# Both heads of a RWKV-7 mixer side by side on TensorE: row and column tiles grouped over two PSUM banks

## The chip, the cores and the metric

The kernel runs on one core of a Trainium2 chip. The metric is the device time of one execution in microseconds. Three executions are given as times; a further one was profiled.

In the profile, PE is TensorE (matrix products), PEld its weight loads, DVE is VectorE, ACT is ScalarE, POOL is GpSimd and SP is SyncE, which issues most transfers.

## What is computed

A two-layer encoder trunk on a sequence of 1024 frames with 1024 channels. Layer 0 has a mixer of two parallel head groups: eight RWKV-7 heads of width 64 and four gated DeltaNet heads of width 128. Layer 1 has chunked softmax attention. Each layer then has a squared-ReLU MLP and a gated embedding. The change touches the mixer of layer 0 alone, and of it the RWKV heads and the triangular inverses that both head groups use. The RWKV part of the reference:

```python
def rwkv7_group(h, dh, r, k, v, ...):
    r, k, v = [z + (token_shift(z) - z) * mu for z, mu in ...]
    w_log = -softplus(-(w0 + tanh(xw @ w1) @ w2)) - 0.5
    decay = exp(-exp(w_log))
    a = sigmoid(a0 + (xa @ a1) @ a2)
    g = sigmoid(xg @ g1) @ g2
    kk = l2norm(heads(k * k_k))
    k = k * (1.0 + (a - 1.0) * k_a)
    y = wkv7_scan(r, decay, k, v, -kk, kk * a)
    ...                                    # group norm, bonus, gate

def step(state, inp):                      # of wkv7_scan, per frame
    r_t, w_t, k_t, v_t, a_t, b_t = inp
    sa = einsum('bhij,bhj->bhi', state, a_t)
    state = state * w_t + sa b_t^T + v_t k_t^T
    return state, einsum('bhij,bhj->bhi', state, r_t)
```

## The kernel before

The scan over frames is done in chunks of 128 frames. Within a chunk everything is matrix products: a strictly lower triangular matrix N from the scaled keys, the inverse of one minus N, three masked score matrices, and a recurrence from chunk to chunk through a state of 64 by 64 for a head.

The work is cut into 16 units: 8 of RWKV and 8 of DeltaNet, in turn. A unit is one half of the sequence (512 frames, four chunks) and, for RWKV, two heads: head 0 lies on partitions 0 to 63 and head 1 on 64 to 127. Each unit goes through stages, each a Python generator: `in` (the wide input projections, out `dps`, from the activations `xg` and the split weights `whi` and `wlo`), `front`, `mid` (the inverse), `back` (scores and recurrence) and `post` (norm and gate). Six lanes run these stages for different units at the same time. `run` picks the lane whose due time is earliest, by the table `LAT` and by a clock `now` that `mm` advances for each product. The tile framework then puts the instructions of each engine in their final order and sets the waits. That order is fixed: PE works through its list strictly in turn.

Names of tiles in the rows, and what they are:

- `wa2` (in rows `wa`) and `lao`: weights and inputs of the two small LoRA products, decay on rows 0 to 63 and `a` on rows 64 to 127. The results are `psw` and `psa`, both in the bank `tp`.
- `AR`, and `Bt`, `Kt` (in rows `b`): scaled rows of both heads. `N` is made of `Bt` and `AR`, one head after the other, in bank `tp`.
- `iz`: the bank of the inverse. Its steps use tiles of 16, 32 and 64 rows: `T` and `X` for the 32-wide step, `TZ` and `F` for the 64-wide step. `N` has eight matrices (four chunks, two heads), DeltaNet's `Ng` four.
- `pm`: the bank of the scores of one head and chunk: three matrices by two products, of 128 and 256 columns. DVE masks them into `PMQ`. The `tm` tiles are transposes of `Bt` and `Kt`.
- `ch`: the bank of the recurrence. For a chunk: `W` from `PMQ` and the state `Sh`; `U` from the inverse `F` and `W`; the new state `S2` from `tm`, `Vt` (in rows `b`) and `U`. DeltaNet's recurrence uses the same bank, with the state `Sg` and the rows `KQ`.
- `py`: the output of the chunk, summed over three parts, the last two per head on 64 output columns of the array.
- `pp`: the bank of the `post` stage (`post_bank`).

Each of these banks is one buffer of 2 KB a partition. A row's `64*128` is the part of the array that a product uses: rows by columns. A product whose operands start at partition 64 uses the array's lower rows, and one whose output starts at partition 64 uses its right columns.

Of the kernel before, what the change touches and what calls it, by code (L numbers as in the profile page):

```python
# [104 lines left out]
class Trunk:  # L105
# [45 lines left out]
    def mm(self, out, lhsT, rhs, start, stop):  # L151
        n, m = 1, 1
        for c in rhs.shape[1:]:
            n *= c
        for c in lhsT.shape[1:]:
            m *= c
        if rhs.dtype == F32:
            self.now += 2 * max(n / 1200, m * 0.0007)
        else:
            self.now += max(n / 2400, m * 0.00035)  # L160
        return self.nc.tensor.matmul(out, lhsT, rhs, start=start, stop=stop)  # L161

    def tr(self, out, in_, ident):
        self.now += 0.107
# [228 lines left out]
    def inverse_end(self, Xp, B, N, F):  # L393
# [8 lines left out]
        def bank(w):  # L402
            return self.psm.tile([P, N, w], F32, tag="iz", name="iz")
# [35 lines left out]
        for i in (0, 2):  # L439
# [4 lines left out]
        yield f"inverse{N}_3"  # L444

        pt = bank(64)
        for g in range(N):
            self.tr(pt[up, g, :], F[up, g, up], self.ident[up, up])
# [2 lines left out]
        A.copy(TZ[up], pt[up])  # L451
        yield f"inverse{N}_4"
        pz = bank(64)
        for g in range(N):
# [4 lines left out]
        for g in range(N):  # L459
            self.mm(px[up, g, :], TZ[lo, g, :], F[lo, g, lo], start=True, stop=True)  # L460
        A.copy(F[up, :, lo], px[up])
        yield f"inverse{N}_6"


# [293 lines left out]
    def rwkv_front(self, p, hf, sc, raws, u):  # L758
# [12 lines left out]
        def ptile():  # L771
            return psm.tile([P, HB], F32, tag="tp", name="tp")
# [10 lines left out]
        A.activation(lw, psw, AF.Tanh, bias=self.dv["hw0"][:, p:p + 1], scale=0.5)  # L783
        V.tensor_scalar(lw, lw, -0.5 * EXPM05, -0.5 * EXPM05, op0=ALU.mult, op1=ALU.add)
# [23 lines left out]
        ta = t2()  # L808
        A.activation(ta, psa, AF.Tanh, bias=self.dv["ha0"][:, p:p + 1], scale=0.5)
        yield "rwkv_front1"  # L810
        pst = ptile()
        for c in range(4):
# [17 lines left out]
            yield ("mid", u - 2)  # L830

        N = self.mid.tile([P, 8, P], F32, tag="n8", name="N")
        for h in range(2):
            sl = slice(64 * h, 64 * h + 64)
            ps = ptile()
            for c in range(4):
                self.mm(ps[:, c * C:(c + 1) * C], Bt[sl, c * C:(c + 1) * C], AR[sl, c, 0, :], start=True, stop=True)
            for c in range(4):
                A.activation(N[:, 4 * h + c, :], ps[:, c * C:(c + 1) * C], AF.Copy, scale=cc[:, 2 * c + h:2 * c + h + 1])
            yield "rwkv_front3"  # L840
        X = self.inverse_start(N, 8)
        V.tensor_tensor(v4(Kt), v4(k2), Em, op=ALU.mult)
        r = mix(0)
# [27 lines left out]
    def rwkv_back(self, p, hf, sc, st, u):  # L871
# [5 lines left out]

        pmq = {}

        def scores(c, h):  # L880

            sl = hs[h]
            ps = psm.tile([P, 3, P], F32, tag="pm", name="pm")
            self.mm(ps[:, 0, :], Bt[sl, c * C:(c + 1) * C], AR[sl, c, 1, :], start=True, stop=True)
            self.mm(ps[:, 1:3, :], Kt[sl, c * C:(c + 1) * C], AR[sl, c].rearrange("p a t -> p (a t)"),
                    start=True, stop=True)
            d = h2.tile([P, 3, P], F32, tag="PMQ", name="PMQ", bufs=NPMQ)
            V.tensor_tensor(d, ps, self.mask3, op=ALU.mult)
            pmq[c, h] = d
# [17 lines left out]
        for c in range(4):  # L907

            Sh = h2.tile([P, 2, 64], F32, tag="Sh", name="Sh", bufs=2)
            V.scalar_tensor_tensor(Sh, S.rearrange("p (o i) -> p o i", o=1).broadcast_to((P, 2, 64)), ee[:, c:c + 1],  # L910
                                   self.blk.rearrange("p (h i) -> p h i", h=2), op0=ALU.mult, op1=ALU.mult)
            if c == 0:
                yield "rwkv_back3"
            Sf = Sh.rearrange("p h i -> p (h i)")
            pw = psm.tile([P, HB], F32, tag="ch", name="ch")
            for h in range(2):
                self.mm(pw[:, hs[h]], pmq[c, h][:, 1, :], Vt[:, c, hs[h]], start=h == 0, stop=False)
            self.mm(pw[:, 0:P], AR[:, c, 0, :], Sf, start=False, stop=True)
# [9 lines left out]
            V.tensor_tensor(U.rearrange("p (h i) -> p h i", h=2), pu[:, 0:P].rearrange("p (h i) -> p h i", h=2),  # L928
                            cc[:, 2 * c:2 * c + 2].rearrange("p (h o) -> p h o", o=1).broadcast_to((P, 2, 64)),
                            op=ALU.mult)  # L930
            yield "rwkv_back5"
# [10 lines left out]
            py_c = py[:, c * C:(c + 1) * C]  # L942
            self.mm(py_c, Sf, AR[:, c, 1, :], start=True, stop=False)
            for h in range(2):
                self.mm(py_c[hs[h]], Vt[:, c, hs[h]], pmq[c, h][:, 2, :], start=False, stop=False)
                self.mm(py_c[hs[h]], U[:, hs[h]], pmq[c, h][:, 0, :], start=False, stop=True)
            yield "rwkv_back6"
        G.tensor_scalar(self.S[f"r{p}"], S, ee[:, 4:5], None, op0=ALU.mult)

# [1004 lines left out]
```

## Time and profile before

| what | value |
|---|---|
| three runs | 3192.11, 3194.34, 3196.0 us (median 3194.34) |
| the profiled execution | 3200.01 us, span 3198.3 us |
| PE busy over the span | 3102.1 us (97%), 17576 records |
| DVE, ACT, POOL busy | 2013.2, 1384.2, 531.5 us |
| the mixer of layer 0 | from the start to about 970 us |
| granted TensorE clock, mean | 0.974 |

The layer 0 mixer takes about 30% of the span; the rest is the output projection, the MLP, the embedding gate and layer 1, which the change leaves alone. Busy time is the time that at least one instruction of the engine is under way. Records of PE overlap their neighbours (a record lasts longer than the distance to the next), so what a product costs is read from the starts.

### The profile page before, as it was taken

Reading aid. Unit: us, or ns where it says so; the run is one execution under the profiler, and the core shown is the slowest. Engines: PE = TensorE matmul, PEld = TensorE weight load, DVE = VectorE, ACT = ScalarE, POOL = GpSimd, SP = SyncE. Lnnn points to the kernel's source line nnn. Section 1 sums busy time; section 2 is a strip of 40 time slices with the busy share of each in tenths; the row PEclk is TensorE's granted clock in tenths of the full one; section 3 lists DMA queues with packets and bytes.
Section 4 is the critical chain, followed back from the end, with each engine's and each line's share of the span. In section 5 each row is a group of like instructions: output and inputs, shape, how many; then the busy total and the mean of one; then the engine's idle time right before and its main releaser. Section 6 shows DMA issues by size and latency. Waiting matters only on the chain.

```text
span 3198.3 us, 46044 instructions
## 1 busy us (share of the span) xinstructions
PE 3102.1 (97%) x17576; PEld 2565.6 (80%) x17576; DVE 2013.2 (63%) x4020; ACT 1384.2 (43%) x2608; POOL 531.5 (17%) x978
## 2 busy tenths in 40 slices
PE   7999999999999999999999898999899999999999
PEld 5777777777777888888888888988778888888887
DVE  6566675556748666655546576776768666655552
ACT  4333333334326555322123477777756555312121
POOL 6334442433410000000004211010110000000002
PEclk8999899999899999999999999999999999999999
DMA  3322112212325433523213210110156433522213
GB/s 120 94 63 60 47 46 67 70 61 70 129 95 194 155 119 108 192 93 106 92 51 128 70 36 32 45 41 16 69 177 209 150 121 109 185 105 92 106 47 105
DMA packets 144716, 309.60 MB, mean 97 GB/s; under 512 B 40944, under 2 KB 43120, under 8 KB 144496
## 3 DMA queue, kind: packets, MB, share of 16 engines
q1 hardware_dynamic: 126064, 273.10, 25.6%
q10 hardware_dynamic: 18432, 33.56, 2.7%
q8 instruction: 138, 2.26, 0.3%
q14 instruction: 82, 0.67, 0.1%
HBM read 232.16 MB, written 74.45 MB: 96 GB/s over the span
## 4 chain that ended last, share of the span: by engine, by line
PE 85%; DVE 7%; ACT 3%; DMA 2%; issue 1%; POOL 0%; SPq 0%; ACTq 0%; DVEq 0%; POOLq 0%
PE dps L161 70%; PE ch L161 3%; PE iz L161 2%; PE pm L161 2%; PE tp L161 1%; PE po L161 1%; PE py L161 1%; DVE ptile L318 1%; PE pt L165 1%; DMA wraw<-in_w_qkv 1%; PE sn L161 1%; PE pp L161 1%; DVE pb L1795 1%; PE sc L161 1%; ACT pb L1808 1%
## 5 line engine op out<-in xcount | busy, mean ns | idle before, releaser
L161 PE MATMUL dps<-r,act 128*128 128x512 f32 x3528 | 824.4, 392 | 0.0
L161 PEld LDWEIGHTS dps<-r,act 128*128 128x128 f32 x3528 | 662.1, 188 | 145.7
L161 PE MATMUL dps<-xg,whi 128*128 128x512 f32 x1280 | 438.2, 418 | 11.7 <-ACT xg L320 7.3
L161 PE MATMUL dps<-late,act 128*128 128x512 f32 x1536 | 352.9, 391 | 0.0
L161 PEld LDWEIGHTS dps<-late,act 128*128 128x128 f32 x1536 | 288.4, 188 | 63.1
L161 PE MATMUL dps<-wq,act 128*128 128x384 f32 x1536 | 304.8, 344 | 5.8 <-DVE vs L1704 3.1
L1452 POOL TENSOR_TENSOR pn<-pn,prs 128x512 f32<-128x512 f32 x32 | 45.5, 1426 | 1590.7 <-ACT prs L354 1496.3
L161 PEld LDWEIGHTS dps<-xg,whi 128*128 128x128 f32 x1280 | 248.4, 199 | 75.2 <-issue 10.7
L161 PEld LDWEIGHTS dps<-wq,act 128*128 128x128 f32 x1536 | 265.6, 191 | 10.4 <-DVE vs L1704 5.1
L161 PE MATMUL dps<-xg,wlo 128*128 128x512 f32 x640 | 266.4, 416 | 3.1 <-DVE wlo L277 3.1
L1328 DVE TENSOR_TENSOR late<-late,dps 128x512 f32<-128x512 f32 x224 | 152.9, 685 | 150.1 <-PE dps L161 119.2
L1427 DVE TENSOR_TENSOR xw<-xw,dps 128x512 f32<-128x512 f32 x192 | 131.5, 685 | 148.4 <-PE dps L161 145.5
L1226 ACT CAST act<-act 128x1024 fp32r<-128x1024 f32 (+1 forms) x99 | 94.8, 964 | 285.2 <-DMA act<-in_w 124.2
L1226 ACT CAST act<-late 128x512 fp32r<-128x512 f32 x210 | 124.5, 618 | 135.9 <-PE dps L161 117.0
L1227 DVE TENSOR_TENSOR act<-late,act 128x512 fp32r<-128x512 f32 x210 | 139.9, 687 | 26.1 <-ACT act L1226 25.9
L161 PEld LDWEIGHTS dps<-xg,wlo 128*128 128x128 f32 x640 | 126.9, 198 | 34.1 <-issue 4.8
L161 PE MATMUL dps<-xw,act 128*128 128x512 f32 x576 | 138.9, 392 | 0.0
L276 ACT CAST whi<-wraw 128x1024 fp32r<-128x1024 f32 x78 | 81.7, 1047 | 124.2 <-PE dps L161 74.4
L161 PEld LDWEIGHTS dps<-xw,act 128*128 128x128 f32 x576 | 108.1, 188 | 24.1
L1227 DVE TENSOR_TENSOR act<-act 128x1024 fp32r<-128x1024 f32 (+1 forms) x99 | 109.9, 1115 | 21.0 <-ACT act L1226 19.8
L161 PE MATMUL po<-ptile,vs 128*128 128x256 f32 (+1 forms) x576 | 104.9, 297 | 17.1 <-DVE ptile L318 7.7
L277 DVE TENSOR_TENSOR wlo<-wraw,whi 128x1024 fp32r<-128x1024 f32 x78 | 101.4, 1301 | 25.6 <-ACT whi L276 25.6
(472 smaller groups left out, 5369.4 us busy)
## 6 DMA issues: line engine op xcount, KB each, us to landing
act<-in_w SPq DMA_DIRECT2D x68, 512.0 KB
hd<-late ACTq DMA_DIRECT2D x128, 256.0 KB
late<-in_w SPq DMA_DIRECT2D x60, 512.0 KB
wraw<-in_w_in SPq DMA_DIRECT2D x56, 512.0 KB
act<-hd SPq DMA_DIRECT2D x56, 512.0 KB
wraw<-in_w_out SPq DMA_DIRECT2D x21, 512.0 KB
wraw<-in_w_qkv SPq DMA_DIRECT2D x21, 512.0 KB
pn<-pnd SPq DMA_DIRECT2D x32, 256.0 KB
```

What stands on the lines that cost most here:

```text
L161: return self.nc.tensor.matmul(out, lhsT, rhs, start=start, stop=stop)
L165: return self.nc.tensor.transpose(out, in_, ident)
L276: nc.scalar.copy(hi, raw)
L277: nc.vector.tensor_tensor(lo, raw, hi.bitcast(F32), op=ALU.subtract)
L318: nc.vector.tensor_tensor(dst[:, 1, sl], src, dst[:, 0, sl].bitcast(F32), op=ALU.subtract)
L1226: A.copy(hi, s)
L1227: V.tensor_tensor(lo, s, hi.bitcast(F32), op=ALU.subtract)
L1328: V.tensor_tensor(r, t, u, op=ALU.add)
L1427: V.tensor_tensor(x[n][:, sl], x[n][:, sl], ps, op=ALU.add)
L1452: G.tensor_tensor(pn, pn, prs[:, sl], op=ALU.mult)
L1795: V.tensor_tensor_reduce(S, pn[:, 0:nn * P], toep[:, (3 - nn) * P:], op0=ALU.add, op1=ALU.max, scale=1.0, scalar=NEG, accum_out=mx[:, 0:1])
L1808: A.activation(S, S, AF.Exp, bias=mx[:, 2:3], accum_out=l[:, 0:1])
```

## The change

Products that use different parts of the array are issued in turn, so that they can be under way together.

- `together` ties a list of products in order (an ordering edge without a semaphore).
- The two LoRA products become one pair: `psa` (rows 64 to 127) goes to the bank `pp` and `psw` to `tp`. The stop `rwkv_front0` goes.
- N of both heads becomes one tied group of eight products, head 1 in `pp` and head 0 in `tp`, alternating by chunk. One stop `rwkv_front3` instead of two.
- The scores of a chunk become one tied group for both heads: head 1 in `pp`, head 0 in `pm`. They are all issued at the chunk before, after its state; before, head 0's came after `W` and head 1's after the state. The stop `rwkv_back0` goes.
- The state and the output products of a chunk are written head by head within each step, and the output's first part comes before the stop `rwkv_back5`.
- In the inverse, the 32-wide step alternates its two tiles, and the 64-wide step puts every other matrix in the upper half of the bank. Its result is then copied by two ACT instructions (even and odd matrices) instead of one.

The number of products, their shapes and their precision stay as they were.

```diff
+    def together(self, products):
+        edge = mybir.DependencyInfo(mybir.DependencyClass.NoSync, mybir.DependencyReason.DATA)
+        for u, v in zip(products, products[1:]):
+            self.tc.add_manual_dep(v.ins, u.ins.name, edge, reason="together")
...
-        for i in (0, 2):
-            for g in range(N):
+        for g in range(N):
+            for i in (0, 2):
                 self.mm(pz[quad[i + 1], g, :], B[quad[i], g, quad[i + 1]], T2[quad[i], g, :], start=True, stop=True)
...
+        def both(ps, f):
+            for g in range(N):
+                f(ps[up if g % 2 == 0 else lo, g, :], g)
+        def out(dst, ps):
+            for e, r in ((0, up), (1, lo)):
+                A.copy(part(dst, e), part(ps[r], e))
...
         pz = bank(64)
-        for g in range(N):
-            self.mm(pz[lo, g, :], B[up, g, lo], TZ[up, g, :], start=True, stop=True)
-        A.copy(TZ[lo], pz[lo])
+        both(pz, lambda o, g: self.mm(o, B[up, g, lo], TZ[up, g, :], start=True, stop=True))
+        out(TZ[lo], pz)
...
-        psw = ptile()
-        self.mm(psw, self.wa2[0:64, p * P:(p + 1) * P], sc["lwa"][0:64], start=True, stop=True)
+        psw, psa = ptile(), self.post_bank()
+        self.together([self.mm(ps, self.wa2[r, p * P:(p + 1) * P], sc["lwa"][r], start=True, stop=True)
+                       for ps, r in ((psa, slice(64, 128)), (psw, slice(0, 64)))])
...
-        yield "rwkv_front0"
-        psa = ptile()
-        self.mm(psa, self.wa2[64:128, p * P:(p + 1) * P], sc["lwa"][64:128], start=True, stop=True)
...
-        for h in range(2):
-            sl = slice(64 * h, 64 * h + 64)
-            ps = ptile()
+        pn = [ptile(), self.post_bank()]
+        ms = []
+        for c in range(4):
+            for h in (1, 0):
+                sl = slice(64 * h, 64 * h + 64)
+                ms.append(self.mm(pn[h][:, c * C:(c + 1) * C], Bt[sl, c * C:(c + 1) * C], AR[sl, c, 0, :],
+                                  start=True, stop=True))
+        self.together(ms)
...
-        def scores(c, h):
...
+        def scores(c):
+            cs = slice(c * C, (c + 1) * C)
+            ps = [psm.tile([P, 3, P], F32, tag="pm", name="pm"), self.post_bank()[:, 0:3 * C].rearrange("p (a t) -> p a t", a=3)]
+            ms = [self.mm(ps[h][:, 0, :], Bt[hs[h], cs], AR[hs[h], c, 1, :], start=True, stop=True) for h in (1, 0)]
+            ms += [self.mm(ps[h][:, 1:3, :], Kt[hs[h], cs], AR[hs[h], c].rearrange("p a t -> p (a t)"),
+                           start=True, stop=True) for h in (1, 0)]
+            self.together(ms)
+            for h in (1, 0):
+                d = pmq[c, h] = h2.tile([P, 3, P], F32, tag="PMQ", name="PMQ", bufs=NPMQ)
+                V.tensor_tensor(d, ps[h], self.mask3, op=ALU.mult)
-        scores(0, 0)
-        yield "rwkv_back0"
-        scores(0, 1)
+        scores(0)
...
-            if c < 3:
-                scores(c + 1, 0)
...
-            for h in range(2):
-                self.mm(pu2[hs[h], 0:64], Ktm[:, c, hs[h]], Vt[:, c, hs[h]], start=True, stop=False)
-                self.mm(pu2[hs[h], 0:64], Btm[:, c, hs[h]], U[:, hs[h]], start=False, stop=True)
+            for t, v in ((Ktm, Vt[:, c]), (Btm, U)):
+                for h in range(2):
+                    self.mm(pu2[hs[h], 0:64], t[:, c, hs[h]], v[:, hs[h]], start=t is Ktm, stop=t is Btm)
+            for v, j in ((Vt[:, c], 2), (U, 0)):
+                for h in range(2):
+                    self.mm(py_c[hs[h]], v[:, hs[h]], pmq[c, h][:, j, :], start=False, stop=j == 0)
...
             if c < 3:
-                scores(c + 1, 1)
+                scores(c + 1)
```

More of the change, by code (lines that the diff above doesn't have):

```diff
@@ L438, in inverse_end @@
         px = bank(32)
-        for i in (0, 2):
-            for g in range(N):
+        for g in range(N):
+            for i in (0, 2):
                 self.mm(px[quad[i], g, :], Z[quad[i + 1], g, :], X2[quad[i + 1], g, :], start=True, stop=True)
@@ L444, in inverse_end @@
         yield f"inverse{N}_3"
+        part = lambda t, e: t[:, e::2, :]
+        def both(ps, f):
+            for g in range(N):
+                f(ps[up if g % 2 == 0 else lo, g, :], g)
+        def out(dst, ps):
+            for e, r in ((0, up), (1, lo)):
+                A.copy(part(dst, e), part(ps[r], e))
         pt = bank(64)
@@ L453, in inverse_end @@
         pz = bank(64)
-        for g in range(N):
-            self.mm(pz[lo, g, :], B[up, g, lo], TZ[up, g, :], start=True, stop=True)
-        A.copy(TZ[lo], pz[lo])
+        both(pz, lambda o, g: self.mm(o, B[up, g, lo], TZ[up, g, :], start=True, stop=True))
+        out(TZ[lo], pz)
         yield f"inverse{N}_5"
         px = bank(64)
-        for g in range(N):
-            self.mm(px[up, g, :], TZ[lo, g, :], F[lo, g, lo], start=True, stop=True)
-        A.copy(F[up, :, lo], px[up])
+        both(px, lambda o, g: self.mm(o, TZ[lo, g, :], F[lo, g, lo], start=True, stop=True))
+        out(F[up, :, lo], px)
         yield f"inverse{N}_6"
@@ L832, in rwkv_front @@
         N = self.mid.tile([P, 8, P], F32, tag="n8", name="N")
-        for h in range(2):
-            sl = slice(64 * h, 64 * h + 64)
-            ps = ptile()
+        pn = [ptile(), self.post_bank()]
[7 more added lines that the diff above has]
+        for h in (1, 0):
             for c in range(4):
[L837 to L840, printed above, removed]
+                A.activation(N[:, 4 * h + c, :], pn[h][:, c * C:(c + 1) * C], AF.Copy, scale=cc[:, 2 * c + h:2 * c + h + 1])
+        yield "rwkv_front3"
         X = self.inverse_start(N, 8)
@@ L878, in rwkv_back @@
         pmq = {}
-        def scores(c, h):
[L882 to L889, printed above, removed]
-        scores(0, 0)
-        yield "rwkv_back0"
-        scores(0, 1)
+        def scores(c):
[5 more added lines that the diff above has]
+            self.together(ms)
+            for h in (1, 0):
+                d = pmq[c, h] = h2.tile([P, 3, P], F32, tag="PMQ", name="PMQ", bufs=NPMQ)
+                V.tensor_tensor(d, ps[h], self.mask3, op=ALU.mult)
+        scores(0)
         yield "rwkv_back1"
@@ L930, in rwkv_back @@
                             op=ALU.mult)
+            py_c = py[:, c * C:(c + 1) * C]
+            self.mm(py_c, Sf, AR[:, c, 1, :], start=True, stop=False)
             yield "rwkv_back5"
             pu2 = psm.tile([P, HB], F32, tag="ch", name="ch")
-            for h in range(2):
-                self.mm(pu2[hs[h], 0:64], Ktm[:, c, hs[h]], Vt[:, c, hs[h]], start=True, stop=False)
-                self.mm(pu2[hs[h], 0:64], Btm[:, c, hs[h]], U[:, hs[h]], start=False, stop=True)
+            for t, v in ((Ktm, Vt[:, c]), (Btm, U)):
[4 more added lines that the diff above has]
+                    self.mm(py_c[hs[h]], v[:, hs[h]], pmq[c, h][:, j, :], start=False, stop=j == 0)
             S2 = h2.tile([P, 64], F32, tag="S2", name="S2", bufs=2)
@@ L940, in rwkv_back @@
             if c < 3:
-                scores(c + 1, 1)
[L942 to L946, printed above, removed]
+                scores(c + 1)
             yield "rwkv_back6"
```

4 lines of the change are left out of this document (2 added, 2 removed).

## The prediction

> **What bounds the kernel now.** I read the page first. TensorE (PE) is busy for 97% of the span, so the page alone says only that the matrix engine's list sets the end.
>
> ```profile
> span 3198.3 us, 46044 instructions
> PE 3102.1 (97%) x17576; PEld 2565.6 (80%) x17576; DVE 2013.2 (63%) x4020; ACT 1384.2 (43%) x2608; POOL 531.5 (17%) x978
> ```
>
> The change touches only the mixer of layer 0, which ends near 970 us. So the second view is the busy time by stretch: length, then PE, PE's weight loads, VectorE (DVE), ScalarE (ACT), GpSimd (POOL), and then the granted clock.
>
> ```profile
> 120.00:970.00 850.00, 831.76 (x6666) 649.86 (x6665) 525.76 (x1220) 309.76 (x626) 316.12 (x700) 0.94 0.23 72
> 970.00:3198.00 2228.00, 2168.98 (x10486) 1837.29 (x10484) 1418.86 (x2686) 1028.64 (x1907) 149.07 (x128) 0.99 0.30 105
> ```
>
> In the mixer's 850 us PE idles 850 - 832 = 18 us, while the other engines have much room. PE's list is the bound: a microsecond off it is a microsecond off the end, as long as no wait takes its place. The granted clock is 0.94 here against 0.99 later.
>
> The third view is the groups of PE instructions by form (count, busy us, mean ns of one). A float32 product is two records.
>
> ```profile
> L161 PE MATMUL pm<-AR,b 64*128 64x256 f32 x128 | 40.3, 395 | 0.0
> L161 PE MATMUL pm<-AR,b 64*128 64x128 f32 x128 | 31.3, 325 | 0.5 <-DVE PMQ L888 0.5
> L161 PE MATMUL tp<-AR,b 64*128 64x128 f32 x128 | 19.8, 295 | 1.5 <-DVE cc L815 1.5
> L161 PE MATMUL tp<-lao,wa 64*128 64x512 f32 x32 | 18.0, 641 | 0.5 <-ACT f L783 0.4
> L161 PE MATMUL iz<-X,T 32*32 32x32 f32 x384 | 17.4, 199 | 0.0
> L161 PE MATMUL iz<-T,N 32*32 32x32 f32 x256 | 9.8, 193 | 0.0
> L161 PE MATMUL iz<-T,Ng 32*32 32x32 f32 x128 | 4.9, 194 | 0.0
> L161 PE MATMUL iz<-F,TZ 64*64 64x64 f32 x192 | 14.7, 222 | 0.0
> L161 PE MATMUL iz<-TZ,N 64*64 64x64 f32 x128 | 9.3, 221 | 0.0
> L161 PE MATMUL iz<-TZ,Ng 64*64 64x64 f32 x64 | 6.0, 237 | 0.0
> ```
>
> These are what the change regroups: the scores (pm, 64 head groups of four records), the matrix N (tp from AR), the two small LoRA products (tp from lao) and the inverses' last steps (iz). Each uses a part of the array.
>
> What two parts do side by side, PE's timeline shows at 577 us (start, time from first start to last end, count). There a LoRA product on rows 64 to 127 of the array happens to stand beside a score group on rows 0 to 63, in another bank.
>
> ```profile
> 576.69 0.51 PE L161 MATMUL iz<-F,TZ 64*64 64x64 f32 x6
> 577.13 0.69 PE L161 MATMUL tp<-lao,wa 64*128 64x512 f32 x1
> 577.13 0.70 PE L161 MATMUL pm<-AR,b 64*128 64x128 f32 x3
> ...
> 578.18 0.50 PE L161 MATMUL dps<-xg,whi 128*128 128x512 f32 x1
> ```
>
> Both start at 577.13, and the next wide product starts 1.05 us later. That is what the two LoRA records need alone (18.0 us for 32, so 1.1 for two). The score group cost nothing: the change's mechanism, in the kernel before.
>
> **What it takes off PE's list.** The prices are read from PE's timeline at 922 and at 904 us.
>
> ```profile
> 922.26 0.40 PE L161 MATMUL dps<-xg,wlo 128*128 128x512 f32 x1
> 922.49 0.62 PE L161 MATMUL dps<-xg,whi 128*128 128x512 f32 x2
> 923.05 0.92 PE L161 MATMUL pm<-AR,b 64*128 64x128 f32 x4
> 923.90 0.59 PE L161 MATMUL iz<-T,Ng 32*32 32x32 f32 x16
> 924.41 0.50 PE L161 MATMUL dps<-xg,wlo 128*128 128x512 f32 x1
> 924.75 0.40 PE L161 MATMUL dps<-xg,whi 128*128 128x512 f32 x1
> 925.08 0.34 PE L161 MATMUL ch<-b,tm 128*64 128x64 f32 x4
> 925.24 0.29 PE L161 MATMUL ch<-U,tm 128*64 128x64 f32 x4
> 925.36 0.28 PE L161 MATMUL py<-PMQ,U 128*64 128x128 f32 x1
> ...
> 925.59 0.38 PE L161 MATMUL py<-PMQ,U 128*64 128x128 f32 x2
> 925.90 0.50 PE L161 MATMUL dps<-xg,whi 128*128 128x512 f32 x1
> ```
>
> ```profile
> 904.03 1.14 PE L161 MATMUL iz<-F,TZ 64*64 64x64 f32 x16
> 905.10 0.49 PE L161 MATMUL py<-AR,Sh 128*128 128x128 f32 x2
> ```
>
> Wide records follow each other at 0.23 us (922.26 to 922.49). The group at 923.05 starts 0.10 late after the second one of 922.49, lasts 0.85 to the next start, and the first wide product after a change of tile size takes 0.34 (924.41 to 924.75), 0.11 too long. So a head's scores cost 0.10 + 0.85 + 0.11 = 1.06 us.
>
> 1. Scores: 64 x 1.06 = 68 us now, 32 pairs x 1.06 = 34 then. In the order, 18 of the 32 pairs stand whole. The other 14 have something else inside, mostly behind head 1's first product, which then pays its own entry, exit and two records, some 0.4 us each, 6 in all. It saves 28.
> 2. N: 19.8 us in 16 head groups, half of it goes: 10.
> 3. LoRA: 1.1 us each, seven of eight pairs adjacent: 8, less 2 for places like 577 us: 6.
> 4. The output py: after the pairing, head 1's last two records no longer run alone. They start at 925.59, and the 0.31 to 925.90 less 0.09 of a change is 0.22, times 32 chunks: 7.
> 5. The inverses' 64-wide steps: 16 records take 1.07 us (904.03 to 905.10), so about 0.058 each without the change. 384 records are 22 us; run on two column halves, 11 go.
> 6. The 32-wide steps: 16 records take 0.51 (923.90 to 924.41), 0.024 each without the change. Alternating tiles I take at two thirds, 0.016; 768 records: 6.
>
> Sum 68 us. With tails and shared changes counted otherwise I get 58 to 78. The count of tile-size changes in PE's order agrees in direction: 632 before, 515 after, up to the mixer's end.
>
> First place of the order: N of the second RWKV unit on PE, before (head 0's four products with one bank; head 1's stand 16 rows on).
>
> ```order
> L161 MATMUL dps<-xg,wlo 128x512
> L161 MATMUL tp<-AR,b 128x128 x4
> L161 MATMUL ch<-W,F_224 128x64 x2
> L161 MATMUL iz<-T_1742,Ng 32x16 x16
> L161 MATMUL dps<-xg,whi 128x512 x2
> ```
>
> The same unit on PE after, head 1 in the bank pp and head 0 in tp.
>
> ```order
> L161 MATMUL iz<-TZ,N 64x64 x8
> L161 MATMUL pp<-AR,b 128x128
> L161 MATMUL tp<-AR,b 128x128
> L161 MATMUL pp<-AR,b 128x128
> L161 MATMUL tp<-AR,b 128x128
> L161 MATMUL pp<-AR,b 128x128
> L161 MATMUL tp<-AR,b 128x128
> L161 MATMUL pp<-AR,b 128x128
> L161 MATMUL tp<-AR,b 128x128
> L161 MATMUL dps<-xg,whi 128x512 x2
> ```
>
> The heads now alternate, so each product has its partner beside it.
>
> **What it gives back: waits.** The answers of DVE, ACT and POOL stay as long as they were. Where PE's own work between a product and the reader of its result was a score group, that cover shrinks. Second place: PE in the recurrence of the third chunk of the second RWKV unit, before.
>
> ```order
> L161 MATMUL pm<-AR,b 128x128
> L161 MATMUL pm<-AR,b 128x256
> L161 MATMUL ch<-Sh,AR 128x128
> L161 MATMUL py<-AR,Sh 128x128
> L161 MATMUL py<-PMQ,b 64x128
> L161 MATMUL ch<-W,F_224 128x64 x2
> L161 MATMUL pm<-AR,b 128x128
> L161 MATMUL pm<-AR,b 128x256
> L161 MATMUL ch<-b,tm 64x64
> L161 MATMUL ch<-U,tm 64x64
> ```
>
> The same chunk on PE after.
>
> ```order
> L161 MATMUL pp<-AR,b 128x256
> L161 MATMUL pm<-AR,b 128x256
> L161 MATMUL ch<-b,tm 64x64 x2
> L161 MATMUL ch<-U,tm 64x64 x2
> L161 MATMUL py<-PMQ,U 64x128 x2
> L161 MATMUL ch<-b,PMQ 128x64 x2
> L161 MATMUL ch<-Sh,AR 128x128
> L161 MATMUL py<-AR,Sh 128x128
> L161 MATMUL py<-PMQ,b 64x128 x2
> L161 MATMUL ch<-W,F_224 128x64 x2
> L161 MATMUL ch<-b,tm 64x64 x2
> L161 MATMUL ch<-U,tm 64x64 x2
> ```
>
> Before, a score group stands between the product that makes U (ch from W and F) and the rows that need U (ch from b and tm, ch from U and tm). After, nothing does. What that costs, the trace shows at 943 us, where it happens once already.
>
> ```profile
> 943.40 0.66 PE L161 MATMUL ch<-W,F 128*128 128x64 f32 x4
> 944.44 0.34 PE L161 MATMUL ch<-b,tm 128*64 128x64 f32 x4 [0.38 <-DVE U L928]
> ```
>
> The four records take 0.11 each, so of the 1.04 us some 0.55 is lost. I went through the five kinds of recurrence step of both head groups in both orders and priced PE's work between maker and reader with the rows above. Steps with under 0.8 us of cover: 12 before, 42 after. So 30 x 0.55 = 16 us come back for certain. The recurrences are about 210 of PE's 656 rows that wait for another engine. If the others lose cover alike, it is 16 x 656 / 210 = 51. I take 40, nearer to the upper end, because the others include two new kinds of wait: the one bank pp now serves the post stage, the second LoRA product, N and the scores, and PE, strictly in order, holds all wide products behind a row that waits for pp's last reader (VectorE's masks and the post stage's products); and the inverse's copies are split in two.
>
> **The clock.** In the mixer the clock is at half for a part of the time, as the busy time by stretch shows.
>
> ```profile
> 538.00:541.40 3.40, 3.40 (x71) 2.94 (x74) 2.44 (x17) 1.75 (x3) 0.45 (x2) 1.00 0.49 154
> 541.40:544.80 3.40, 3.40 (x25) 2.35 (x24) 3.12 (x20) 0.37 (x1) 2.18 (x5) 0.50 0.02 5
> 544.80:548.20 3.40, 3.40 (x9) 2.35 (x8) 1.45 (x3) 0.00 (x0) 0.70 (x1) 0.50 0.00 0
> ```
>
> ```profile
> 546.72 0.63 PE L161 MATMUL dps<-xg,wlo 128*128 128x512 f32 x1
> 547.15 1.05 PE L161 MATMUL dps<-xg,whi 128*128 128x512 f32 x2
> ```
>
> Wide records then follow at 0.43 instead of 0.23, so one such stretch of 3.4 us costs 1.7. The stretch before the drop (538.00) has PE busy for all 3.40 us, but with small tiles. More waits make more lean stretches, shorter small-tile runs make fewer. I take 5 more, 8 us, between 0 and 10 more (17 us). [...]
>
> Costed at nothing: the tie itself (no instruction), the split copies (ACT works 310 of 850 us; uncovered, 32 x 0.15 would be 5 us, which the 51 holds), and the front's removed stops. N's transfer on SP's queue waits for the same eight ACT copies as before.
>
> **The sum.** -68 + 40 + 8 = -20 us. The profiled execution took 3200.0 us, its span 3198.3. It lies 0.2% over the median of the runs, 3194.3, so I take the difference from that median: 3174.
>
> **The rivals.**
> A, the waits eat it. Place: PE rows that wait for the bank pp and the recurrences. Price 0.55 us each; beyond 110 new waits, 60 us, the gain is gone. With 75 us it ends at 3194 - 68 + 75 + 8 = 3209. For it: 658 of PE's rows wait for another engine after the change, and no wide product can pass one of them. Against: PE idles only 18 us now. Chance 0.13.
> B, the waits stop at the counted 16 and the clock stays: -52, 3142. For it: most steps in the order still have over 2 us of cover. Chance 0.15.
> C, column halves of one row range don't overlap, so terms 4 and 5 fail: -68 + 18 + 40 + 8 = -2, 3192. Against: at 925.08 eight column-half records take 0.28 us to 925.36, half of eight times 0.058. [...] Chance 0.05.
> D, row halves pair at 577 us but not when both load 128 columns at each step: terms 1 to 3 shrink to the saved tile-size changes, about 20, with 24 from the rest; then the new order's waits (40) and the clock (17) win: +13, 3207. For it: no row shows two such streams in step. Chance 0.04.
>
> **How the numbers follow.** The forecast, 3174, has 0.63, with a range of its own of 3158 to 3190. A measurement of this kernel can tell about 0.2%, 6 us, from no change. Faster: 0.60 of the forecast's 0.63 and B's 0.15, with a bit of C: 0.76. Same: C and the forecast's edge, 0.09. Slower: A and D, less their near edges: 0.15. The range reaches to near B's 3142, at 3145, and on the other side to 3200, short of A and D.
>
> **What would show it.** Right: score, N and LoRA groups of both heads within one run of about 1.06, 1.2 and 1.1 us, two records starting together; PE's busy time in the mixer down by 30 us or more while its idle time rises from 18 to 30 or more; waits of half a microsecond for U, W, S2 and pp. Wrong: pairs that last twice as long (D), 64-wide steps still at 0.058 a record (C), idle time under 25 us (B) or over 70 (A).

## The result: slower by 0.9%, and the profile after

The changed kernel takes 3224.8 us (median of six executions, 3215.1 to 3233.2) against 3193.6 us for the kernel before (six executions, 3192.1 to 3196.1). The ratio is 1.0089, with a 95% interval of 1.0073 to 1.0105. The forecast was 3174, in a range of 3145 to 3200: wrong, and wrong in sign. The profiled execution took 3223.7 us, its span is 3222.0 us.

The head of the page after, span and engines, answers the first fence of the prediction. PE is still busy nearly throughout, but by 43 us less.

```profile
span 3222.0 us, 46099 instructions
PE 3059.5 (95%) x17576; PEld 2537.6 (79%) x17576; DVE 2011.8 (62%) x4020; ACT 1389.1 (43%) x2640; POOL 528.5 (16%) x978
```

The busy time by stretch, the mixer after 120 us and the rest of the span: first the kernel before.

```profile
120.00:967.00 847.00, 830.98 (x6664) 649.36 (x6663) 523.67 (x1217) 309.14 (x625) 316.12 (x700) 0.94 0.23 72
967.00:3198.00 2231.00, 2169.76 (x10487) 1837.80 (x10486) 1420.95 (x2688) 1029.26 (x1908) 149.07 (x128) 0.99 0.30 105
```

The same two stretches after; the mixer now ends at 992 us.

```profile
120.00:992.00 872.00, 793.98 (x6679) 621.78 (x6677) 522.61 (x1217) 314.66 (x657) 313.41 (x700) 0.90 0.23 70
992.00:3222.00 2230.00, 2168.15 (x10487) 1840.51 (x10486) 1419.62 (x2688) 1028.89 (x1908) 147.03 (x128) 0.99 0.31 105
```

The rest of the span is as long as it was (2231 and 2230 us). All the loss is in the mixer, 25 us longer, and it can be split in three. PE's idle time rises from 847 - 831 = 16 us to 872 - 794 = 78 us, by 62. The granted clock falls from 0.94 to 0.90: by the clock records of the two traces it is at half for 101 us before and 172 after. Of these, PE is idle for 7 and 26 us, which stand in the idle time already. In the other 95 and 147 us it works at half clock and loses half of them, 47 and 73 us, so 26 more. What is left, PE's own work at full clock, falls from 784 to 721 us. So 25 = -63 + 62 + 26, where the prediction had -68 + 40 + 8. The change took off nearly what it was to take off, and the two terms that give back were both too small.

The -63 is seen in PE's timeline after (start, time to the last end). First a LoRA pair, then the scores of both heads.

```profile
271.99 0.69 PE L161 MATMUL pp<-lao,wa 64*128 64x512 f32 x1
271.99 0.69 PE L161 MATMUL tp<-lao,wa 64*128 64x512 f32 x1
...
273.05 0.44 PE L161 MATMUL iz<-T,Ng 32*32 32x32 f32 x16
273.89 0.37 PE L161 MATMUL pp<-AR,b 64*128 64x128 f32 x1 [0.40 <-ACT f L798]
273.89 0.37 PE L161 MATMUL pm<-AR,b 64*128 64x128 f32 x1
...
274.74 1.05 PE L161 MATMUL tp<-hsel,f 128*128 128x2 f32 x8
```

Both LoRA products take 273.05 - 271.99 = 1.06 us, as one did before, and both heads' scores 274.74 - 273.89 = 0.85, the time of one head. The partners start together to 0.01 us. Column halves run side by side too, in the inverse's 64-wide step:

```profile
358.68 0.68 PE L161 MATMUL iz<-TZ,N 64*64 64x64 f32 x16
359.29 0.51 PE L161 MATMUL dps<-xg,whi 128*128 128x512 f32 x1
```

Sixteen records take 0.61 us, where 1.07 stood before. Rivals C and D are out.

The 62 us of idle time, in the view of PE's waits after (from 120 us to the mixer's end: total, times, longest):

```profile
PE iz L161 <- ACT T L416: 11.4, 7, 3.3
PE ch L161 <- DVE U L941: 10.1, 10, 2.3
PE ch L161 <- DVE S L957: 5.0, 12, 1.4
PE ch L161 <- DVE Sg L1128: 4.6, 5, 2.4
PE ch L161 <- DVE Sh L925: 4.5, 5, 1.3
```

U, the states S, Sg and Sh are the recurrence, as foreseen, but a wait for U is 1.0 us long (10.1 / 10); at the place that the prediction took its price of 0.55 from, the row shows 0.38. The longest was not foreseen: the first step of an inverse, which waits for `T`. The timeline of all engines shows such a place.

```profile
257.06 0.60 POOL L392 COPY sub<-sub 32x256 f32<-32x256 f32 x1
...
257.69 0.33 SPq L394 DMA_DIRECT2D z<-sub  x1
...
258.44 1.05 PE L161 MATMUL pp<-ones,o 128*128 128x1 f32 x8 [1.17 <-ACT o L1135]
...
259.36 0.47 PE L161 MATMUL py<-AR,Sh 128*128 128x128 f32 x2
259.37 0.37 SPq L396 DMA_DIRECT2D Xp<-z  x1
...
262.43 0.35 ACT L416 ACTIVATE T<-Xp,half 128x64 f32<-128x64 f32 x1 [3.52 <-DMA Xp<-z]
262.83 0.63 PE L161 MATMUL iz<-T,Ng 32*32 32x16 f32 x32 [3.01 <-ACT T L416]
263.39 1.22 PE L161 MATMUL dps<-xg,whi 128*128 128x512 f32 x2
264.41 0.63 PE L161 MATMUL dps<-xg,wlo 128*128 128x512 f32 x1
264.84 1.05 PE L161 MATMUL dps<-xg,whi 128*128 128x512 f32 x2
```

POOL ends the small 16-wide inverses at 257.66, two transfers carry them through memory to 262.4, and PE, which got there early, stands for 3.0 us with wide products next in its list. Then the wide products run at 0.43 us each (264.41 to 264.84). The busy time of these stretches shows why:

```profile
256.50:259.90 3.40, 2.10 (x14) 1.71 (x14) 1.38 (x4) 1.61 (x4) 1.02 (x3) 1.00 0.29 70
259.90:263.30 3.40, 0.47 (x32) 0.47 (x32) 2.49 (x14) 0.35 (x1) 0.46 (x1) 0.52 0.40 123
263.30:266.70 3.40, 3.40 (x21) 2.69 (x13) 0.00 (x0) 0.31 (x1) 0.00 (x0) 0.50 0.00 0
```

In the first, PE works 2.1 of 3.4 us, 0.9 us of it on the one-column products of 258.44; the clock falls in the second and still holds PE back in the third, which is full. So this wait is paid twice, once as 3.0 us of idle time and once in the clock behind it (0.43 us a wide product instead of 0.23). Counted from the clock records after 100 us, the mixer falls to half clock 14 times before and 22 times after.

### The profile page after: what moved, and what is told of

Same layout as the page of the kernel before. It is cut to its first block, busy times and chain, and to the rows that moved or that the text cites. A ratio compares the mean times of both kernels' runs of the same rounds, so it can differ in the third digit from the quotient of the medians.

```text
span 3222.0 us, 46099 instructions
## 1 busy us (share of the span) xinstructions
PE 3059.5 (95%) x17576; PEld 2537.6 (79%) x17576; DVE 2011.8 (62%) x4020; ACT 1389.1 (43%) x2640; POOL 528.5 (16%) x978
## 4 chain that ended last, share of the span: by engine, by line
PE 73%; DVE 9%; ACT 4%; DMA 4%; POOL 2%; issue 2%; SPq 0%; DVEq 0%; POOLq 0%; ACTq 0%
PE dps L161 63%; PE ch L161 2%; PE po L161 1%; PE pp L161 1%; PE iz L161 1%; POOL subt L389 1%; PE pt L171 1%; DVE ptile L324 1%; PE sn L161 1%; DMA wraw<-in_w_qkv 1%; POOL sub L391 1%; DMA Xp<-z 1%; DVE pb L1809 1%; ACT pb L1822 1%; DMA yr<-yd 1%
## 5 line engine op out<-in xcount | busy, mean ns | idle before, releaser
L161 PE MATMUL dps<-xg,whi 128*128 128x512 f32 x1280 | 445.4, 425 | 23.7 <-ACT xg L326 7.5
```

## Experiments

For every execution there is a time, a span and a mean granted clock. So a time can be split without a trace: span x (1 - clock) is what the half clock costs at most (idle time at half clock counts in it), and the remainder of the median time is called rest. The columns are medians of each version. The ratio is to executions of the kernel before that ran beside that version; the row before has the 31 that ran beside e1 to e4. PE's idle time is that of the mixer in the profiled execution, good to some 3 us by where its end is set, and the profiled execution is not always a typical one (3185 us for e1, 3221 for e3).

| version | us | ratio to before, 95% | clock | half clock costs | rest | idle |
|---|---|---|---|---|---|---|
| before | 3197.0 | 1 | 0.973 | 86 | 3111 | 16 |
| the change | 3224.8 | 1.0089 (1.0073 to 1.0105) | 0.9575 | 137 | 3088 | 78 |
| e1 inverses alone | 3196.7 | 1.0000 (0.9987 to 1.0014) | 0.972 | 89 | 3107 | 21 |
| e2 LoRA and N alone | 3200.5 | 1.0011 (0.9995 to 1.0027) | 0.9695 | 98 | 3103 | 19 |
| e3 scores alone | 3212.5 | 1.0044 (1.0029 to 1.0060) | 0.9675 | 104 | 3108 | 38 |
| e4 state and output alone | 3204.9 | 1.0023 (1.0010 to 1.0036) | 0.971 | 93 | 3112 | 24 |
| e5 head after head | 3226.4 | 1.0097 (1.0077 to 1.0116) | 0.9605 | 127 | 3099 | 60 |
| e6 filler | 3209.0 | 1.0047 (1.0029 to 1.0065) | 0.970 | 96 | 3113 | 57 |
| e7 N, inverses, state | 3166.2 | 0.9910 (0.9893 to 0.9928) | 0.9745 | 81 | 3085 | 27 |
| e8 scores in tp | 3191.9 | 0.9976 (0.9959 to 0.9993) | 0.965 | 112 | 3080 | 54 |
| e9 old scores | 3203.3 | 1.0017 (1.0006 to 1.0029) | 0.9625 | 120 | 3083 | 30 |
| e10 pairs behind W, in tp | 3163.5 | 0.9900 (0.9885 to 0.9915) | 0.9715 | 90 | 3073 | 39 |
| n1 before, other order | 3196.5 | 1.0000 (0.9990 to 1.0009) | 0.975 | 80 | 3117 | 19 |
| e11 e9 with the stop | 3176.1 | 0.9936 (0.9917 to 0.9955) | 0.9685 | 100 | 3076 | 24 |
| e12 e7 without the stop | 3178.1 | 0.9942 (0.9923 to 0.9960) | 0.970 | 95 | 3083 | 21 |
| e13 before with filler | 3213.4 | 1.0056 (1.0031 to 1.0080) | 0.975 | 80 | 3133 | 23 |
| e14 e10, other order | 3162.0 | 0.9893 (0.9872 to 0.9914) | 0.971 | 92 | 3070 | 34 |
| e15 change with the stop | 3228.9 | 1.0104 (1.0074 to 1.0134) | 0.958 | 136 | 3093 | 68 |
| e16 e10 in pp | 3197.8 | 1.0007 (0.9984 to 1.0029) | 0.966 | 109 | 3089 | 61 |

**The parts by themselves (e1 to e4).** Each puts one part of the diff into the kernel before: e1 the hunks of `inverse_end`, e2 those of LoRA and N, e3 `scores` and its calls, e4 the lines from `py_c` to `S2`.

> The kernel before with the change to the inverses alone (32-wide steps alternate, 64-wide steps on two column halves, split copies). Two theories for the 30 us by which the whole change is slower. Cover theory: the groups save what the prediction took, and the loss comes from the recurrence steps that lost their cover and from the shared bank pp, so not from here: 3194 - 17 = 3177, at most 5 more for the split copies. Order theory: any edit that puts PE's list in a new order costs some 25 us of waits and half clock, wherever the edit is: 3194 - 17 + 25 = 3202.

> The kernel before with the LoRA pair and the group of N alone (both in banks tp and pp, two stops gone). Cover theory: -16 and some waits for pp, 3180 to 3188. Order theory: -16 + 25, 3203.

> The kernel before with the paired scores alone (both heads after the chunk's state, banks pm and pp). Cover theory: nearly all the loss is here, -28 + 55 = +27, 3221. Order theory: -28 + 25, 3191.

> The kernel before with the new order of the state's and the output's products alone (scores stay head by head at their old places). Cover theory: -7 and a little given back, 3187 to 3191. Order theory: -7 + 25, 3212.

Both theories fell. Cover fits e3 roughly (3212) but not e1 (3197), order fits e2 (3200) and not e3, and neither fits e4 (3205). No part gains. They add 0, 3, 16 and 8 us, 27 together, about what the whole loses. The split shows what they share: the half clock costs more in each (3, 12, 18, 7 us) while the rest hardly falls. Yet each part does take off what it should. Split like the mixer above, by the clock records of the profiled executions, PE's work at full clock falls by 13, 15, 25 and 11 us in e1 to e4, where the prediction had 17, 16, 28 and 7. These add up to 64, and the whole change takes off 63. So the savings add, and in each part waits and clock took them back. From here on the clock was the first theory.

**Unpairing in place (e5).** The scores, and N in the same way:

```diff
-            ms = [self.mm(ps[h][:, 0, :], Bt[hs[h], cs], ...) for h in (1, 0)]
-            ms += [self.mm(ps[h][:, 1:3, :], Kt[hs[h], cs], ...) for h in (1, 0)]
+            ms = []
+            for h in (1, 0):
+                ms += [self.mm(ps[h][:, 0, :], ...), self.mm(ps[h][:, 1:3, :], ...)]
```

> The changed kernel with the products of the scores and of N tied head after head instead of in turn (all of head 1, then all of head 0); banks, places and everything else as in the change. Time is split here into a part at full clock (time less span times one minus the mean granted clock) and the rest, which the half clock costs. Changed kernel: 3225, of it 3089 and 136. Pairs save: the full-clock part rises by the 28 + 10 us that the prediction gave to scores and N, to 3127, and the total to 3255 to 3270. Pairs save nothing: no change, 3225.

It gave 3226, the rest 11 us more. That is no answer to whether pairs save, because the edit did not unpair. PE's timeline of e5 for N, where all four products of head 1 (pp) are listed ahead of head 0's (tp):

```profile
292.90 0.82 PE L161 MATMUL pp<-AR,b 64*128 64x128 f32 x5
293.45 0.37 PE L161 MATMUL tp<-AR,b 64*128 64x128 f32 x1
293.56 0.27 PE L161 MATMUL pp<-AR,b 64*128 64x128 f32 x1
...
293.89 0.72 PE L161 MATMUL tp<-AR,b 64*128 64x128 f32 x5
294.54 0.49 PE L161 MATMUL py<-AR,Sh 128*128 128x128 f32 x2
```

Head 0's first record starts at 293.45, ahead of head 1's sixth at 293.56: here PE starts a product ahead of three records that stand before it in the list and use the other rows. The group takes 1.64 us. In the change it takes 1.09, as its timeline shows.

```profile
292.86 0.37 PE L161 MATMUL pp<-AR,b 64*128 64x128 f32 x1
292.87 0.37 PE L161 MATMUL tp<-AR,b 64*128 64x128 f32 x1
...
293.95 0.34 PE L161 MATMUL ch<-U,tm 128*64 128x64 f32 x4
```

The scores, four records a head, ran as pairs as before.

**The clock: filler (e6, e13).** Added work that nobody reads, behind U's product:

```diff
             for h in range(2):
                 self.mm(pu[:, hs[h]], X[:, 4 * h + c, :], W[:, hs[h]], start=True, stop=True)
+            nc.tensor.matmul(pu[:, P:3*P], self.ident, self.mask3[:, 0:2, :], start=True, stop=True)
```

> The changed kernel with added work: behind each RWKV product that makes U, one float32 product of the full array, 128 by 256, into unused columns of the bank ch, read by no one: 32 x 0.44 = 14 us more for PE. Clock theory (half clock follows stretches in which the array does little, and is the main loss): granted clock up from 0.958 by 0.003 or more, and the time no longer than 3225 in spite of the work. Waits theory (the loss is idle time): the filler stands in the waits for U, 10 us, the rest is added: 3229 with the clock as it was.

> The kernel before with the same filler as in the changed kernel (32 float32 products of the full array behind U's products, 14 us of work that nobody reads). Clock theory: where scores stand behind U already, the clock has less to gain: full-clock part up by 14 to 20, half-clock share down by 5 to 15, so 3197 to 3211, no gain as in the changed kernel (-16). If the filler helps for another reason: 3180 or less.

With 14 us more to do, the changed kernel is 16 us faster (3209; the two ratios' intervals do not touch): the half clock costs 96 us instead of 137, the rest is 25 longer. Idle time at half clock is in the 41 us between them. Split by the clock records of the two profiled executions, PE's work rises by 23 us, its idle time falls by 21 (the waits for U from 10.1 to 4.6, those for `T` from 11.4 to 3.0), and the half clock while PE works costs 17 less. So work can buy back both losses here, and the clock is not the whole gain. In the kernel before, the same filler costs 16 us, a little more than expected, and the clock has only 6 to give. The filler can move the order too, so the gain need not come from the filled waits alone.

**The clock by itself (c_clock).** Ahead of the kernel before, stretches of float32 products of the full array: 128-column ones ("wide") mixed evenly with one-column ones, then chains of wide products that wait for ScalarE. `product` issues one of them and ties it to the one before.

```diff
+for share in (12, 9, 7, 5):
+    for i in range(110):
+        if (i + 1) * share // 20 > i * share // 20:
+            product(d[:, 0:P], self.ones)
+        else:
+            product(t[:, 0:1], self.ones[:, 0:1])
+    dense(50)
+for k in (4, 2, 1):
+    x = self.ones
+    for _ in range(96 // (k + 2)):
...
+        for _ in range(k):
+            product(d[:, 0:P], x)
...
+        nc.scalar.copy(x, d[:, 0:P])
+    dense(50)
```

> The kernel before with a row of test stretches on PE ahead of everything, some 250 us: products of the full array, 128 by 128 columns, mixed evenly with products of one column, PE busy throughout, with shares of 60, 45, 35 and 25% of the wide ones; then chains of 4, 2 and 1 wide products, each chain waiting for ScalarE's copy of its result, so with gaps well under 1 us and PE in use for about two thirds, a half and a third; 50 wide products between stretches. Activity theory: the clock is granted in full at 60% and two thirds, and falls to half at 25% and at a third; the border shows where. [...]

One execution took 3520 us. The busy time by stretch; the clock is the number behind POOL's.

```profile
18.00:42.00 24.00, 24.00 (x216) 24.00 (x216) 0.00 (x0) 1.56 (x3) 0.00 (x0) 1.00 0.07 23
54.00:77.00 23.00, 23.00 (x208) 23.00 (x208) 0.00 (x0) 0.00 (x0) 0.00 (x0) 1.00 0.01 1
...
93.60:137.70 44.10, 44.10 (x208) 44.10 (x209) 0.00 (x0) 0.00 (x0) 0.00 (x0) 0.50 0.00 1
148.00:187.00 39.00, 39.00 (x200) 39.00 (x199) 0.00 (x0) 0.00 (x0) 0.00 (x0) 0.54 0.00 0
202.00:225.00 23.00, 16.95 (x118) 14.10 (x118) 0.00 (x0) 3.98 (x15) 0.00 (x0) 1.00 0.00 1
238.00:250.00 12.00, 7.70 (x44) 5.61 (x44) 0.00 (x0) 2.65 (x10) 0.00 (x0) 1.00 0.00 0
251.00:270.00 19.00, 14.48 (x51) 11.24 (x51) 0.00 (x0) 3.12 (x12) 0.00 (x0) 0.50 0.00 0
286.00:315.00 29.00, 20.13 (x52) 12.76 (x52) 0.00 (x0) 6.62 (x25) 0.00 (x0) 0.50 0.00 1
```

In the first four rows PE is busy throughout. With 60 and 45% of wide products the clock is granted in full. With 35% it is at half from 93.6 us on (the stretch began at 89.2), and with 25% soon too. A record takes 24.0 / 216 = 0.111 us. So the chains of four wide products use the array for 118 x 0.111 / 23 = 57% and keep the clock. Those of two use it for 44 x 0.111 / 12 = 41%, with gaps of only (12 - 7.7) / 11 = 0.4 us; they keep it for 12 us and lose it between 250 and 251 us. Those of one run at half clock. So in this run the border lies between 35 and 45% where the rest is thin work, and below 57% where it is idle time. The clock records place it more closely. In them the clock changes only at steps of 3.41 us (so too in the traces before and after), and in such steps the chains of two start 13, 12, 12 and 11 records: it falls after the one with 11 (11 x 0.111 / 3.41 = 36%), not after 12 (39%). The stretch of 35% has 11 wide records in the step before its fall. In these falls PE has no gap, or gaps of 0.4 us.

Much the same border is found in the mixer. For each step of 3.41 us at full clock, PE's records were added up, each at the time measured for its columns (0.111 us for 128, or 0.23 us for 512 in the wide projections) times the share of the array's rows and columns that it uses. This was done in the traces of both kernels and of all other versions, from 100 us to near the mixer's end. Of the 311 steps after which the clock fell, 298 use under 37% of the array; of the 3684 after which it stayed, 32 do. Without the share of rows and columns the two kinds mix: the best border then has 141 steps on the wrong side, and 41 with it. The traces of before and after alone have 36 such falls, 34 of them under 37%, and 398 steps after which the clock stayed, 4 of them; the best border there has 15 steps on the wrong side without the share, and 3 with it.

**Which part brings it: scores (e7 to e10, e16).** e7 has N, the inverses and state and output changed, scores and LoRA as before; e9 adds the LoRA pair, with the stop `rwkv_front0` gone as in the change; e8 is the change with the LoRA products as before and

```diff
-            ps = [psm.tile([P, 3, P], F32, tag="pm", name="pm"), self.post_bank()[...]...]
+            ps = [psm.tile([P, 3, P], F32, tag="pm", name="pm"), psm.tile([P, HB], F32, tag="tp", name="tp")[...]...]
```

e10 is e8 with the call moved, and e16 is e10 with `post_bank()` again.

```diff
             A.copy(W, pw[:, 0:P])
+            if c < 3:
+                scores(c + 1)
...
             S = S2
-            if c < 3:
-                scores(c + 1)
```

> The change without its scores part and without the LoRA pair (both as before): paired N, the inverses and the new order of state and output. If the parts simply add up as measured one by one (inverses -1, N and LoRA +3, state and output +8): 3204 to 3208. If the loss sits in the paired scores' place and bank and in the LoRA pair's earlier start: -10 -17 -7 on PE's list with some 12 us of waits: 3175.

> The change with head 1's scores in the bank tp instead of pp, and the LoRA products apart as before. Shared-bank theory (pp, which the post stage, N and the scores share, makes the waits that bring the half clock): the waits shrink by 15 to 20 us and the clock recovers to 0.967 or more, 3185 to 3200. If the place of the scores behind the state is what matters, not the bank: 3215 to 3225.

> The changed kernel with its scores part undone (head by head, head 0's after W, head 1's after the state, bank pm); N, LoRA, inverses, state and output stay changed. If the scores' new place and bank make the loss: near the version without the LoRA pair, 3166 to 3178, granted clock 0.972 or more. If the LoRA pair and its earlier start hold a part of it: 3185 to 3200.

> The change with the paired scores of the next chunk issued right after W's product (where head 0's were before), head 1's in the bank tp, and the LoRA products apart as before. Cover theory: the pair hides W's copy again and the waits fall below the 54 us of the version with the pair behind the state (3192): clock 0.970 or more, 3160 to 3180. If the pair's place does not matter, 3185 to 3195.

> The version with the paired scores behind W's product and the LoRA products apart (3163.5), with head 1's scores in the bank pp, as in the change, instead of tp. If the place decides: 3160 to 3172. If the shared bank pp makes waits of its own: 3180 to 3200.

e7 is 31 us faster than before, though the inverses alone gained nothing, state and output alone lost 8, and N, measured only together with LoRA, lost 3 with it. PE's work falls by 39 us, about what these parts take off; the half clock while PE works costs no more than before (43 and 47 us). So the savings add, and what waits and clock take back does not. Place and bank of the paired scores are separate effects, some 30 us each: behind W instead of behind the state 3192 to 3164, bank tp instead of pp 3198 to 3164. PE's waits in e16:

```profile
PE pp L171 <- DVE o L985: 5.0, 3, 1.9
PE pp L171 <- DVE fr L1154: 5.0, 2, 2.7
PE ch L161 <- DVE U L945: 4.0, 10, 0.5
...
PE pp L161 <- DVE PMQ L908: 2.1, 2, 1.5
```

and in e10:

```profile
PE ch L161 <- DVE U L945: 3.0, 7, 0.8
...
PE pp L161 <- DVE o L991: 1.5, 2, 1.2
...
PE pp L161 <- ACT o L1137: 1.2, 1, 1.2
```

Products into pp wait 12 us in the three rows of e16, under 3 in the two of e10 (over all rows for pp, 14 and 4). Of the 12 us, 10 are waits of the post stage for its own next operand, and 2 for the mask that still reads the bank. The first step of an inverse waits 7.3 us for `T` in e16 and 0.6 in e10. So the bank costs 34 us, but mostly not as waits for the bank itself. That sharing it brings the two stages' chains close together in PE's list would explain it, and is not shown.

Against e7, whose scores stand as before, e10 gains only 3 us, less than the intervals can tell. In the profiled executions its pairs take 24 us off PE's work, and 12 us of idle time and 15 of half clock come back.

**LoRA and the stop (e11, e12, e15).** One line is put back behind the LoRA pair in e9 (e11) and in the whole change (e15), and taken out of e7 (e12).

```diff
+        yield "rwkv_front0"
```

> The version with the scores as before and everything else changed (3203, of it 3082 at full clock and 120 for the half clock), with the planner's stop rwkv_front0 put back behind the LoRA pair's readers. If the dropped stop (the front stage's steps run earlier and leave lean stretches) brings the half clock: 3165 to 3180, half-clock share 80 to 95. If the pair itself does, by waiting for the bank pp: 3195 to 3205.

> The version with the scores and the LoRA products as before (3166, of it 3087 and 80), with the stop rwkv_front0 taken out and nothing else. Stop theory: 3185 to 3200, the rise in the half-clock share. Bank theory: 3163 to 3172.

> The changed kernel with the planner's stop rwkv_front0 put back, one line, nothing else. With the scores as before this line was worth 27 us (3203 to 3176). If it works the same way here: 3195 to 3205, the gain in the half-clock share. If the scores behind the state bring most of the half clock by themselves: 3212 to 3225.

With old scores, the pair with its stop costs 10 us over e7 (3176), the missing stop alone 12 (3178), both together 37 (3203). Nearly all of it is half clock (100, 95 and 120 us against 81); the idle time hardly moves (24, 21 and 30 us against 27). In the whole change the stop brings nothing back (3229): the expectation failed. The mixer falls to half clock 23 times with it and 22 without. Why that is so, and why pair and missing stop together cost more than their sum, stays open.

**Order alone (n1, e14).** Three numbers of LAT changed, in the kernel before and in e10.

> The kernel before with three numbers of the table LAT changed (inverse8_3 0.58 to 0.49, inverse8_5 0.82 to 0.94, rwkv_back1 1.11 to 1.28): the same products, banks and groups in another order. Order theory: another order alone moves the time by 5 us or more, all of it in the half clock, while the part at full clock stays within 3 us of 3113. Otherwise 3194 to 3200.

> The fastest version so far (paired scores behind W's product, head 1 in bank tp, LoRA apart; 3163.5, of it 3074 and 90) with three numbers of LAT changed (gdn_scalars1 4.26 to 3.62, gdn_front5 1.56 to 1.79, gdn_front2 0.81 to 1.22), the same products in another order. If its gain hangs on one order: 3175 or more. If it is the pairs and the cover: 3155 to 3170, the full-clock part within 4 of 3074.

Neither moves (3196.5 and 3162.0). So it is not any other order that costs; with one order tried each, that is a sample and not a proof. e14 is the fastest version: 1.1% under the kernel before.

## Why the prediction was wrong

- **What it takes off PE's list**: right. -68 was forecast, in 58 to 78, and the mixer gives -63. Pairs of scores (0.85 us), of N (1.09 for both heads) and of LoRA (1.06) ran in the time of one, and sixteen records on column halves took 0.61 us, where 1.07 stood before.
- **What it gives back, waits**: a step that failed. 40 with a bound of 51, measured 62. The price of 0.55 came from one short wait for U; ten such waits now take 1.0 us each. The step also missed that PE, with a shorter list, also arrives early at chains that were hidden before: POOL and two transfers ahead of an inverse, up to 3.3 us at a time. The criterion set for rival A, idle time over 70 us, is met (850 - 778 = 72 us up to 970 us of the profile after). A had 0.13 and 3209; it has the waits, but left the clock at 8 us.
- **The clock**: the step that failed most for its size. 8 us with a bound of 17, measured 26 in the profiled mixer, and at most 137 - 86 = 51 by the medians, with idle time at half clock counted in. Five more half-clock stretches of 3.4 us were assumed; (172 - 101) / 3.4 is 21. The prediction had read the mechanism (the drop without a gap at 538 us), but priced waits and clock apart. A wait lowers the use of a stretch that small tiles have already made lean. In the traces, 298 of 311 falls came after a step of under 37%, and at least the next 3.41 us then ran at half speed. So a wait of half a microsecond that tips such a step costs over two (0.5 + 1.7), an estimate from these figures.
- **The sum**: -68 + 40 = -28 was forecast without the clock, and -63 + 62 = -1 came. The waits took the whole saving, and the clock made the loss. So the sign needed both errors.
- **The bank pp** was named, as a wait of some 0.5 us. e16 against e10 shows 34 us for it, 19 of them half clock.

## What to carry to other kernels

Count the clock as a resource of its own: in this mixer, whose clock fell after stretches of 3.4 us with under some 37% of full array use, a regrouping that took 63 us off PE's work gave back 62 in waits and 26 in half clock, and the mean granted clock of each execution hinted at it without a trace (0.9575 against 0.973). Pair products through banks that no other stage's chain holds, and leave them where they hide another engine's answer (3164 against 3192 and 3198 us). Test parts in company as well as alone: here none of the four parts gained by itself, while N, the inverses, and state and output together gained 31 us.

## What was not expected of the hardware

- The granted clock fell to half with PE busy without a gap, at 35% wide products and not at 45%. Chains at 41% with gaps of 0.4 us lost it too, after 12 us.
- In the mixer, the falls of the clock stand apart best when each product is counted with the share of the array's rows and columns that it uses: counted so, 298 of 311 falls come after 3.41 us with under 37% of use, and the best border has 41 steps on the wrong side instead of 141.
- 14 us of added work made the changed kernel 16 us faster, and the kernel before 16 us slower.
- A product of head 0 started ahead of three records of head 1 that stand before it in the list (293.45, then 293.56). So "strictly in turn", as is said of PE ahead of the prediction, does not hold there for products on different rows. By their start times at least 18 of the 17576 records of the kernel before, and 204 of the changed kernel, stand elsewhere than in the program's list, all of them products on a part of the array.
- The spread between executions of one kernel is mostly the clock: the six of the change lie from 3215 us (clock 0.961) to 3233 us (0.955). The profiled one is an exception, with 3224 us at 0.961.
